# Row factors stored to DRAM in 20-byte runs or as one run, with natural rows interleaved by five

## The chip, the cores and the metric

One core of one Trainium2 chip runs the kernel. The metric is the device time of one execution in microseconds (us).

## The reference

The kernel computes one inference step of a one-layer hybrid decoder with 4096 prompt tokens and 64 sample tokens of width 1024. Only the first lines matter for the change:

```python
def _rmsnorm(x, g):
    xf = x.astype(jnp.float32)
    r = lax.rsqrt(jnp.mean(xf * xf, axis=-1, keepdims=True) + RMS_EPS)
    return (xf * r).astype(x.dtype) * g
...
    h = _rmsnorm(x, g_pre)
    z = h @ w_in
    cb, cc, ch, cg, q, k, v, ag, mq, mg = _split_cols(z)
```

Every token has one factor r, from the sum of its squares; h is the token times r times a gain per channel; z is its projection to 2816 columns. Three groups work on z (a gated short convolution, sliding-window attention with sinks, attention to 256 memory tokens); an output projection and a second norm follow.

## The kernel before

The 4160 tokens (64 of the sample, then 4096 of the prompt) are cut into eight blocks of 520. The input projection runs in three phases, each over all eight blocks and about one third of the columns. Products are made of f32 operands split into a high and a low part (`split`, L360 and L361; `product`, L370), blocks 0 and 1 of phase 0 by plain block products, the rest by a scheme of seven products in place of eight. The inputs x come transposed (`x_load`, L240): channels lie on partitions and tokens along the free axis.

**Row factors.** A sum over channels would be a sum over partitions there, so the factors come from a second read of x in natural order. A block has five tiles `nat` of 104 tokens by 1024 channels (`row_load`, L264 to L267, on the SP queue). `row_step` squares one tile on ScalarE and adds it up along the row (L278) into one column of a small tile `r` of 104 partitions by 5. After the fifth, GpSimd makes the five columns into factors (L284, L285). Column i, partition p belongs to token 104 i + p of the block.

The factors are wanted along the free axis, the same on all 128 partitions. There are two ways to it. Blocks 0 and 2 (`PLAIN_BLOCKS` is 2) go through TensorE: `rows_diag` spreads the factors over the diagonals of a tile (L297), `rows_product` multiplies it by ones (L306), and ScalarE copies the bank to a tile `rb` (L308). Blocks 1 and 3 to 7 go through DRAM: GpSimd stores `r` to `rowd` (L290), and four steps later `rows_load` on the SP queue reads it back to all partitions at once (L253). Block 0 is stored to `rowd` too: phase 1 reads `rowd` again for blocks 0 and 1.

VectorE multiplies by `rb`: the inputs (`scale`, L337), whose results are stored for the later phases; for blocks 0 and 1 it does that only in phase 1, and in phase 0 it multiplies their outputs z (L625).

**Order of the work.** The whole projection is recorded with the order of each engine as the program writes it. All of SP's loads stand in one queue and start in order. GpSimd issues in the first phase all stores (`store`, L166): the gates `md`, the attention operands `qd`, the scaled inputs `hd`, and the `rowd` stores among them. A store of GpSimd also waits for the store issued eight places before it, whose semaphore it takes over.

Of the kernel before, what the change touches and what calls it, by code (L numbers as in the profile page):

```python
# [20 lines left out]
NS = 64  # L21
# [23 lines left out]
PLAIN_BLOCKS = 2  # L45
# [7 lines left out]
def hybrid_layer(ctx: ExitStack, tc: tile.TileContext, a: dict):  # L53
    nc = tc.nc
    TE, V, S, G, DMA = nc.tensor, nc.vector, nc.scalar, nc.gpsimd, nc.sync
# [17 lines left out]
    rowd = [tc.dram_tile([2 * HW], F32, name=f"rowd{b}") for b in range(NBLK)]  # L73
# [170 lines left out]
    RG = 104  # L244

    rows = {}
    nat, sq, after_nat = {}, [0], [14]

    row_loads, row_spreads = [], {}

    def rows_load(b, again=False):
        rows[b] = (temp(f"rb{b}")[:, : 2 * HW] if again else natp.tile([P, 2 * HW], F32, tag="rb", name=f"rb{b}"))
        DMA.dma_start(rows[b], rowd[b].partition_broadcast(P))  # L253

    def row_load(j):
        if j < 5 * NBLK:
            g = RG * j - NS
            if 2 <= j < 10 or 12 <= j < 14:
                t = (wa if j < 7 or j == 12 else wb).tile([P, 2, 512], F32, tag="w", name=f"nat{j}")
                t = nat[j] = t.rearrange("p a n -> p (a n)")  # L260
            else:
                t = nat[j] = natp.tile([P, D], F32, tag="nat", name=f"nat{j}")
            if g < 0:
                DMA.dma_start(t[:NS], a["x_s"])  # L264
                DMA.dma_start(t[NS:RG], a["x_p"][: RG - NS, :])
            else:
                DMA.dma_start(t[:RG], a["x_p"][g : g + RG, :])  # L267

    def row_step():

        j = sq[0]
        if j == 5 * NBLK:
            return
        b, i = divmod(j, 5)
        if i == 0:
            nat["r"] = tiny.tile([P, 8], F32, tag="r", name=f"r{b}", bufs=3)
        r, t = nat["r"], nat.pop(j)
        S.activation(t[:RG], t[:RG], AF.Square, accum_out=r[:RG, i : i + 1])  # L278
        if j in (10, 11) or j >= 14:
            row_loads.append(after_nat[0])  # L280
            after_nat[0] += 1
        sq[0] += 1
        if i == 4:
            G.tensor_scalar(r[:RG, 0:5], r[:RG, 0:5], 1.0 / D, EPS, op0=ALU.mult, op1=ALU.add)  # L284
            G.tensor_tensor(r[:RG, 0:5], r[:RG, 0:5], mhalf[:RG, 0:5], op=ALU.pow)  # L285
            if b in (0, PLAIN_BLOCKS):
                nat["factors"] = r
            if b == PLAIN_BLOCKS:
                return
            G.dma_start(rowd[b].rearrange("(i p) -> p i", p=RG), r[:RG, 0:5])  # L290
            if b > 0:
                row_spreads[b] = 4

    def rows_diag():

# [6 lines left out]
    def rows_product(b):  # L302

        acc = rows[b]
        for half in range(2):
            TE.matmul(acc[:, half], ones[:RG], diag[:RG, HW * half : HW * half + HW], start=True, stop=True)  # L306
        rows[b] = natp.tile([P, 2 * HW], F32, tag="rb", name=f"rb{b}")
        S.copy(rows[b].rearrange("p (a n) -> p a n", a=2), acc)  # L308

    def row_queue():  # L310

        for j in row_loads:
            row_load(j)
        row_loads.clear()
        for b in [b for b, n in row_spreads.items() if n == 1]:
            rows_load(b)
        for b in list(row_spreads):
            row_spreads[b] -= 1
            if row_spreads[b] == 0:
                del row_spreads[b]  # L320
# [229 lines left out]
    def next_block(ph, b, p):  # L550

        nph, nb = (ph, b + 1) if b + 1 < NBLK else (ph + 1, 0)
        load = lambda o: lambda: x_of(nph, nb, o)
        ready = lambda o: lambda: x_ready(nph, nb, o)
        jobs = []
        if nph < 2:
            jobs += {0: "B11", 3: "B21 B12", 4: "B22"} .get(p, "").split() if ph == 0 else \
                    {0: "B11", 3: "B21", 4: "B12", 5: "B22"}.get(p, "").split()
            jobs = [load(o) for o in jobs]
        if ph == 0:  # L560
            jobs.insert(0, row_queue)
            if 1 <= p < 4:
                jobs.append(row_step)
        if p == 1 and nph == 1 and nb < PLAIN_BLOCKS:
            jobs.append(lambda: rows_load(nb, nb > 0))
        if nph < 2:
            jobs += [ready(o) for o in ({4: "B11", 5: "B21 B12", 6: "B22"} if ph == 0 else
                                        {4: "B11", 5: "B21", 6: "B12 B22"}).get(p, "").split()]
        if ph == 0 and 4 <= p < 6:
            jobs.append(row_step)  # L570
        if nph < 2:
            if p == 6:
                jobs.append(lambda: t_sum(nph, nb, "T1"))
        return jobs
# [53 lines left out]
    def plain_jobs(b, s):  # L628
# [16 lines left out]
            (0, 6): lambda: [*parts(1, "B11"), *row, *fills(1, "S1", "S4"), *sums(3, 0), *row],  # L645
            (0, 7): lambda: [*row, *fills(3, "S2", "S3"), lambda: rows_diag()],
            (1, 0): lambda: [*parts(1, "B21"), *row, *row, lambda: rows_bank(0), lambda: rows_product(0), *z_rows(0, 1)],
            (1, 1): lambda: [*z_rows(0, 0), *done(0, 1), *row, *row],
            (1, 2): lambda: [*parts(1, "B12"), *done(0, 0), *fills(3, "S1"), *row],
            (1, 3): lambda: sums(2, 0),  # L650
            (1, 4): lambda: [*row, lambda: rows_diag(), lambda: rows_bank(2), *parts(1, "B22"), *gains(2, "B11"), *sums(2, 1),
                             *fills(2, "S2")],
            (1, 5): lambda: [lambda: rows_product(2), *fills(2, "S3"), *row, *fills(2, "S1"), *gains(2, "B21"), *fills(2, "S4"),
                             *row],
            (1, 6): lambda: [*scales(2, "B11"), *gains(2, "B12"), *scales(2, "B21", "B12"), *row],
# [4 lines left out]
    def plain_loads(b, s):  # L660
        if s + b == 0:
            first_w("A22")
        for j in {(0, 0): (0,), (0, 1): (1,), (0, 2): (2, 3, 4), (0, 3): (5, 6, 7), (0, 4): (8, 9, 10), (0, 5): (11,),
                  (0, 7): (12, 13)}.get((b, s), ()):
            row_load(j)
        if (b, s) == (0, 1):
            first_w("A12")
        for nb, o in {(0, 1): [(0, "B12")], (0, 2): [(0, "B22")], (0, 3): [(1, "B11")], (0, 4): [(1, "B21")],
                      (0, 6): [(1, "B12")], (0, 7): [(1, "B22")], (1, 2): [(2, "B11")], (1, 3): [(2, "B21")],
                      (1, 4): [(2, "B12")], (1, 5): [(2, "B22")]}.get((b, s), ()):  # L670
            x_of(0, nb, o)
        row_queue()
# [1583 lines left out]
```

## Time and profile before

| what | value |
| --- | --- |
| runs | 1472.13, 1472.27, 1476.53 us; median 1472.27 |
| profiled execution, its own time | 1470.74 us |
| span of the profiled execution | 1469.0 us |
| granted TensorE clock | 0.999 of full speed |
| moved by DMA | 369.59 MB, mean 252 GB/s |
| stores to `rowd` | 7, of 2 KB each |

The profile is of one execution. The span runs from the first instruction to the last; the execution's own time is 1.74 us more. Busy time, waits and the chain of waits are read from that one execution: a row with "<-" names an engine and line that waited and what ended the wait; the three numbers behind it are the total in us, how often, and the longest. In rows of a tile, three durations are minimum, median and maximum in ns, with the start of the first and the last in us. In a window's row each engine has busy time and, in brackets, the instructions that touched the window; PE is TensorE, PEld its weight loads, DVE VectorE, ACT ScalarE and POOL GpSimd, and SPq a DMA queue of SyncE.

### The profile page before, as it was taken

What the parts mean: (1) busy time and instruction counts of PE and PEld (TensorE: products, weight loads), DVE (VectorE), ACT (ScalarE), POOL (GpSimd) and SP (SyncE); (2) the same over time, 40 slices, a digit from 0 to 9 for tenths busy, and PEclk for the clock granted to TensorE, in tenths of its full rate; (3) what the DMA queues carried; (4) which work ended last, traced back from release to release, by engine and by line L of the source; (5) the groups of instructions that cost most, each with busy time, mean ns of one, the idle gap of its engine ahead of it and who ended that gap; (6) DMA issues with size and microseconds to landing.
All of it is one profiled execution on the core that took longest, in us unless ns stands there. A gap on an engine that the chain in (4) does not pass through costs nothing.

```text
span 1469.0 us, 31997 instructions
## 1 busy us (share of the span) xinstructions
PE 1453.3 (99%) x11887; PEld 1342.3 (91%) x11887; DVE 1235.0 (84%) x1991; ACT 888.9 (61%) x2170; POOL 431.9 (29%) x544
## 2 busy tenths in 40 slices
PE   9999999999999999999999999999999999999997
PEld 9999999999999999999999999778888888888875
DVE  6779887899988888798677777899998999999975
ACT  6776565566532222244545444788888878888862
POOL 0222322312403474300021130234334333433452
PEclk9999999999999999999999999999999999999999
DMA  9999999887866676688897679997887788888876
GB/s 265 191 248 223 297 275 265 248 288 248 216 229 244 243 248 232 225 284 253 281 233 266 215 215 329 279 280 240 252 263 241 240 243 268 243 248 264 254 266 224
DMA packets 233744, 369.59 MB, mean 252 GB/s; under 512 B 38501, under 2 KB 144485, under 8 KB 233557
## 3 DMA queue, kind: packets, MB, share of 16 engines
q1 hardware_dynamic: 210549, 314.66, 69.4%
q0 software_dynamic: 22320, 51.84, 12.4%
q8 instruction: 94, 1.54, 0.5%
q10 hardware_dynamic: 720, 1.05, 0.2%
q14 instruction: 61, 0.50, 0.1%
HBM read 251.00 MB, written 117.46 MB: 251 GB/s over the span
## 4 chain that ended last, share of the span: by engine, by line
PE 89%; DVE 4%; DMA 3%; ACT 2%; issue 1%; POOL 0%; ACTq 0%; SPq 0%; DVEq 0%; POOLq 0%
PE c L370 54%; PE y_c L1701 20%; PE ws L1394 3%; PE wo L1508 2%; PE wo L1115 2%; PE xs L1441 2%; PE wo L1503 1%; PE wt L1461 1%; PE xt L1461 1%; PE mem_acc L797 1%; DMA md<-th 1%; DMA nat<-in_x_p 1%; DMA ws4A<-in_w_in 1%; PE y L2069 1%; DMA md<-cacc 0%
## 5 line engine op out<-in xcount | busy, mean ns | idle before, releaser
L377 DVE TENSOR_TENSOR z<-c,z 128x520 f32<-128x520 f32 (+1 forms) x308 | 193.8, 643 | 71.8 <-PE c L370 70.8
L1425 ACT ACTIVATE sm<-sm,wnm 128x129 f32<-128x129 f32 x240 | 93.5, 392 | 13.8 <-DVE wrd L1429 7.1
L1701 PE MATMUL y_c<-wob,rows 128*128 128x512 f32 x384 | 95.8, 396 | 0.4 <-ACT s L1739 0.4
L1701 PE MATMUL y_c<-woT,a 128*128 128x512 f32 x384 | 95.2, 395 | 0.0
L1701 PE MATMUL y_c<-woT,down 128*128 128x512 f32 (+1 forms) x396 | 95.2, 389 | 0.0
L1701 PEld LDWEIGHTS y_c<-wob,rows 128*128 128x128 f32 x384 | 70.6, 188 | 17.5 <-ACT wpt L1366 2.4
L1701 PEld LDWEIGHTS y_c<-woT,down 128*128 128x128 f32 x396 | 71.7, 188 | 15.8 <-DVE swnm L1996 0.4
L1701 PEld LDWEIGHTS y_c<-woT,a 128*128 128x128 f32 x384 | 70.6, 188 | 15.2
L1232 ACT ACTIVATE xp<-xs,xnm 128x256 f32<-128x256 f32 x128 | 59.9, 483 | 20.4 <-PE wo L1115 13.5
L918 POOL TENSOR_TENSOR os0T<-os0T,os1T 128x512 f32<-128x512 f32 x20 | 29.0, 1448 | 125.2 <-DMA os1T<-in_w_out 75.8
L411 ACT CAST zh<-z 128x520 fp32r<-128x520 f32 x56 | 33.3, 625 | 40.9 <-DVE z L377 32.9
L1394 PEld LDWEIGHTS ws<-ring,q 128*128 128x128 f32 (+1 forms) x480 | 48.6, 186 | 8.4 <-issue 1.2
L278 ACT ACTIVATE nat<-nat 104x1024 f32<-104x1024 f32 x40 | 42.3, 1057 | 23.0 <-DMA nat<-in_x_p 23.0
L1411 DVE COPY_PREDICATED sm<-wmask,ws 128x512 f32<-128x512 uint8 x60 | 43.7, 754 | 14.6 <-ACT sm L1405 14.6
L1455 ACT ACTIVATE xp<-xp,xrd 128x256 f32<-128x256 f32 x120 | 53.9, 503 | 2.1 <-DVE xrd L1238 1.1
L1394 PE MATMUL ws<-ring,q 128*128 128x256 f32 (+1 forms) x480 | 54.0, 294 | 1.1 <-issue 0.6
L1366 ACT COPY wpt<-wt 128x512 f32<-128x512 f32 x60 | 33.9, 593 | 27.4 <-PE wo L1508 27.4
L379 ACT COPY z<-c 128x520 f32<-128x520 f32 (+1 forms) x44 | 24.2, 553 | 43.0 <-PE c L370 40.0
L1701 PE MATMUL y_c<-woT,diag 128*128 128x512 f32 x192 | 48.8, 400 | 0.0
L1369 POOL TENSOR_SCALAR_AFFINE_SELECT wpt<-wpt 128x512 f32<-128x512 f32 x64 | 46.1, 740 | 7.0 <-ACT wpt L1368 6.9
L1641 POOL TENSOR_TENSOR yst<-yst,mhalf 128x1 f32<-128x1 f32 (+1 forms) x33 | 20.4, 617 | 93.7 <-DVE yst L1640 93.7
L166 POOL DMA_DIRECT2D md<-th x48 | 26.2, 547 | 67.6 <-DVE th L430 59.4
(1055 smaller groups left out, 5537.9 us busy)
## 6 DMA issues: line engine op xcount, KB each, us to landing
woT<-tdT SPq DMA_DIRECT2D x75, 512.0 KB
q<-qd SPq DMA_DIRECT2D x112, 192.0 KB
xr<-in_x_p SPq DMA_DIRECT2D x32, 512.0 KB
nat<-in_x_p SPq DMA_DIRECT2D x39, 416.0 KB
o_yp<-xr SPq DMA_DIRECT2D x31, 512.0 KB
md<-th POOLq DMA_DIRECT2D x48, 260.0 KB, 7.2
qd<-zh SPq DMA_DIRECT2D x48, 260.0 KB
qd<-z SPq DMA_DIRECT2D x42, 260.0 KB
```

The lines of the kernel that those rows point to most:

```text
L278: S.activation(t[:RG], t[:RG], AF.Square, accum_out=r[:RG, i : i + 1])
L370: TE.matmul(bank[:, :HW], l, r, start=first and i == 0, stop=last and i == 3 * KH - 1)
L377: add = lambda dst, other: V.tensor_tensor(dst, c, other, op=ALU.add)
L411: S.copy(hi, z)
L1232: S.activation(p[:, i, :], s[:, i, :], AF.Exp, bias=nm[:, i : i + 1], scale=SCALE, accum_out=den[:, i : i + 1])
L1366: S.copy(p3.rearrange("p h (r q) -> p r h q", r=2), t)
L1369: select = lambda out, step, op, slope: lambda: G.affine_select(out, p3, pattern=[[0, 4], [step, P]], compare_op=op, fill=0.0, base=0, cha ...
L1394: TE.matmul(out(kvh, col, bank), q(kvh, col, bank)[r], k(kvh, part)[r], start=first, stop=True, skip_group_check=not first, **place)
L1411: V.copy_predicated(self.of[i].sms[kvh][:, :, :P].rearrange("p (h a) k -> p a h k", a=2), third["wmask"].unsqueeze(1).to_broadcast([P, 2, ...
L1425: S.activation(sm[:, hh, :], sm[:, hh, :], AF.Exp, bias=nm[:, hh : hh + 1], scale=SCALE, accum_out=den[:, hh : hh + 1])
L1455: S.mul(p[:, i, :], p[:, i, :], self.rds[h][:, i : i + 1])
L1701: TE.matmul(self.acc[bank], self.parts[name][:, l, j], wo[o][j][:, r, cs], start=new and j + i == 0, stop=j == 3 and i == 2, skip_group_ch ...
```

## The change

It has three parts. For blocks 1 and 3 to 7 the five natural tiles no longer hold 104 consecutive tokens each: tile i takes tokens i, i+5, i+10 and so on, so that partition p of `r` holds the factors of the five neighbours 5p to 5p+4, and the store to `rowd` writes 104 runs of 20 bytes where it wrote 520 runs of 4 bytes. Blocks 0 and 2 keep the natural order, since their way through TensorE expects it. Block 0's copy in `rowd` is no longer written from `r` but from the first partition of the spread tile `rb`, as one run of 2080 bytes.

```diff
+    def spread(b):
+
+        return b not in (0, PLAIN_BLOCKS)
+
     def row_load(j):
...
                 DMA.dma_start(t[NS:RG], a["x_p"][: RG - NS, :])
+            elif spread(j // 5):
+                g = 5 * RG * (j // 5) - NS
+                DMA.dma_start(t[:RG], a["x_p"][g : g + 5 * RG, :].rearrange("(p i) d -> p i d", i=5)[:, j % 5])
             else:
                 DMA.dma_start(t[:RG], a["x_p"][g : g + RG, :])
...
-            if b in (0, PLAIN_BLOCKS):
+            if spread(b):
+                G.dma_start(rowd[b].rearrange("(p i) -> p i", i=5), r[:RG, 0:5])
+                row_spreads[b] = 4
+            else:
                 nat["factors"] = r
-            if b == PLAIN_BLOCKS:
-                return
-            G.dma_start(rowd[b].rearrange("(i p) -> p i", p=RG), r[:RG, 0:5])
-            if b > 0:
-                row_spreads[b] = 4
...
         S.copy(rows[b].rearrange("p (a n) -> p a n", a=2), acc)
+        if b == 0:
+            G.dma_start(rowd[b].unsqueeze(0), rows[b][:1])
```

On GpSimd, at the start of the program, before the change (`r0` and `r1` are the factors of blocks 0 and 1, `th` a gate):

```order
L284 TENSOR_SCALAR r0_501<-r0_501 104x5
L285 TENSOR_TENSOR r0_501<-r0_501,mhalf_68 104x5
L290 DMA rowd0_75<-r0_501 104x5x1
L284 TENSOR_SCALAR r1_700<-r1_700 104x5
L285 TENSOR_TENSOR r1_700<-r1_700,mhalf_68 104x5
L290 DMA rowd1_76<-r1_700 104x5x1
L166 DMA md_150<-th0_3_989 128x520
```

And the same place with the change (`rb0` is the spread tile of block 0):

```order
L291 TENSOR_SCALAR r0_501<-r0_501 104x5
L292 TENSOR_TENSOR r0_501<-r0_501,mhalf_68 104x5
L291 TENSOR_SCALAR r1_699<-r1_699 104x5
L292 TENSOR_TENSOR r1_699<-r1_699,mhalf_68 104x5
L294 DMA rowd1_76<-r1_699 104x5
L315 DMA rowd0_75<-rb0_941 13x1x40
L166 DMA md_150<-th0_3_989 128x520
```

Block 0's store has moved behind block 1's factors and their store, directly ahead of block 0's gate stores, and it reads one partition in 13 pieces of 40 numbers.

On GpSimd again, at block 6's factors, the rows before:

```order
L166 DMA hd5_B12_123<-place_160 128x1040
L284 TENSOR_SCALAR r6_2675<-r6_2675 104x5
L285 TENSOR_TENSOR r6_2675<-r6_2675,mhalf_68 104x5
L290 DMA rowd6_81<-r6_2675 104x5x1
L166 DMA md_150<-th4_2_2984 128x520
L166 DMA md_150<-th4_4_3001 128x520
```

And now:

```order
L166 DMA hd5_B12_123<-place_160 128x1040
L291 TENSOR_SCALAR r6_2675<-r6_2675 104x5
L292 TENSOR_TENSOR r6_2675<-r6_2675,mhalf_68 104x5
L294 DMA rowd6_81<-r6_2675 104x5
L166 DMA md_150<-th4_2_2984 128x520
L166 DMA md_150<-th4_4_3001 128x520
```

Nothing has moved here; only the form of the store differs, 104 runs of five numbers in place of 104 by 5 runs of one. On the other engines and on the SP queue the order is as before.

## Prediction

> **What bounds the kernel now.** The page comes first: its head and its row for TensorE.
>
> ```profile
> span 1469.0 us, 31997 instructions
> PE 1453.3 (99%) x11887; PEld 1342.3 (91%) x11887; DVE 1235.0 (84%) x1991; ACT 888.9 (61%) x2170; POOL 431.9 (29%) x544
> ```
>
> TensorE is busy for 1453.3 of 1469.0 us, so the whole kernel has 15.7 us in which it could start work sooner. The change touches only the first stage; the last product with a row factor starts at 382.5 us:
>
> ```profile
> L337 DVE TENSOR_TENSOR place<-place,rb x16: 1224/1233/1245, 94.7 to 382.5; 128x1040 f32<-128x1040 f32 x16
> ```
>
> So the second view is the windows of that stage, with columns for each engine's busy time, its instruction count, the granted clock, the DMA share and GB/s.
>
> ```profile
> core 0: us, PE busy (x) PEld busy (x) DVE busy (x) ACT busy (x) POOL busy (x), PEclk, DMA share, GB/s
> 0.00:20.00 20.00, 18.36 (x128) 17.74 (x129) 11.04 (x20) 11.57 (x22) 0.87 (x8) 1.00 0.90 274
> 20.00:60.00 40.00, 40.00 (x334) 39.88 (x334) 31.61 (x58) 31.74 (x63) 6.30 (x6) 1.00 0.98 221
> ...
> 100.00:140.00 40.00, 39.81 (x334) 39.60 (x334) 38.08 (x45) 27.40 (x49) 13.35 (x20) 1.00 0.93 241
> ...
> 180.00:220.00 40.00, 40.00 (x338) 40.00 (x337) 32.30 (x39) 23.07 (x39) 11.38 (x20) 1.00 1.02 270
> 220.00:260.00 40.00, 39.86 (x335) 39.65 (x333) 32.01 (x39) 24.56 (x43) 12.17 (x21) 1.00 0.99 268
> ...
> 300.00:340.00 40.00, 40.00 (x338) 40.00 (x337) 38.72 (x50) 27.36 (x49) 6.44 (x12) 1.00 0.77 244
> ```
>
> Two things stand here. The DMA engines are full (share 0.93 to 1.02) where the factors are made, which makes a cheaper store look promising. But TensorE does not wait for them: it runs 338 matmuls in 40 us at share 1.02 and the same 338 at share 0.77. What it loses after its start is 0.19 us (100 to 140) and 0.14 us (220 to 260). The waits of TensorE up to 420 us say the same:
>
> ```profile
> PE idle L707 <- POOL ident masks.py:199: 1.6, 1, 1.6
> PE c L370 <- DVE lo_2T L361: 0.2, 1, 0.2
> ```
>
> The 1.6 us lies before the first product and before any row factor exists; it stays.
>
> **The stores that change.** The third view is the tile `rowd`, the DRAM buffer of factors:
>
> ```profile
> L290 POOL DMA_DIRECT2D rowd<-r x7: 989/995/1192, 41.6 to 261.8; - x7
>   POOL md L166: 3.5, 1
> DMA to landing us min/median/max: 9.3/11.8/14.5
> ```
>
> Seven stores of 2 KB, each 520 runs of 4 bytes, take GpSimd about 1 us to issue and 9.3 to 14.5 us to land. Stage windows of 1 us around the store issued at 221.4 show what it does to everything else:
>
> ```profile
> 221.00:222.00 1.00, 1.00 (x11) 1.00 (x10) 0.72 (x2) 1.00 (x4) 0.70 (x2) 1.00 0.82 331
> ...
> 225.00:226.00 1.00, 1.00 (x11) 1.00 (x10) 1.00 (x2) 1.00 (x3) 0.00 (x0) 1.00 0.81 37
> 226.00:227.00 1.00, 1.00 (x11) 1.00 (x10) 1.00 (x2) 0.83 (x3) 0.00 (x0) 1.00 0.11 0
> 227.00:228.00 1.00, 1.00 (x10) 1.00 (x10) 1.00 (x3) 1.00 (x2) 0.42 (x1) 1.00 0.36 21
> 228.00:229.00 1.00, 1.00 (x11) 1.00 (x10) 1.00 (x2) 0.35 (x1) 1.00 (x3) 1.00 0.66 75
> ...
> 233.00:234.00 1.00, 1.00 (x11) 1.00 (x10) 0.99 (x2) 0.67 (x2) 0.72 (x2) 1.00 1.05 376
> ```
>
> From 225 to 229 us the core moves 37, 0, 21 and 75 GB/s where 331 and 376 stand on either side: a hole worth 4 - (37+0+21+75)/354 = 3.6 us of full traffic (354 is the mean of 331 and 376). That the tiny runs make it is my inference from its place, just behind the store; no row of this profile separates it from the transfers around it. TensorE's column stays at 1.00 through all of it.
>
> GpSimd's own timeline and the waits of GpSimd, ScalarE and the SP queue show who suffers:
>
> ```profile
> 221.40 0.99 POOL L290 DMA_DIRECT2D rowd<-r  x1 [0.30 <-POOL r L285]
> 222.39 1.11 POOL L166 DMA_DIRECT2D md<-th  x2
> ...
> 232.65 1.07 POOL L166 DMA_DIRECT2D md<-th  x2 [3.46 <-DMA rowd<-r]
> ```
>
> ```profile
> ACT nat L278 <- DMA nat<-in_x_p: 23.0, 11, 4.8
> ACT th L429 <- DMA md<-th: 16.3, 5, 5.0
> ```
>
> ```profile
> SPq L253 <- DMA rowd<-r: 4.4, 1, 4.4
> ```
>
> And the chain of waits shows how little of that reaches TensorE:
>
> ```profile
> 205.54 9.98 DMA nat<-in_x_p
> ...
> 222.39 10.92 DMA md<-th
> ...
> 233.33 0.30 ACT th L429
> ...
> 249.90 170.10 PE c L370 x1425
> ```
>
> One gate store queued right behind `rowd` takes 10.92 us to land, ScalarE waits for its buffer and goes on at 233.33, and what follows releases TensorE at 249.90. This is the one place where the chain through the factors reaches TensorE, and there it waited no more than the 0.14 us of its window.
>
> **The change part by part.** *Six stores in runs of 20 bytes (blocks 1, 3 to 7).* Runs fall from 520 to 104. For the price per run I take the nearest store of GpSimd, 128 runs of 2080 bytes:
>
> ```profile
> L166 POOL DMA_DIRECT2D md<-th x48 | 26.2, 547 | 67.6 <-DVE th L430 59.4
> ```
>
> ```profile
> md<-th POOLq DMA_DIRECT2D x48, 260.0 KB, 7.2
> ```
>
> (989 - 547) / (520 - 128) = 1.13 ns a run, so 104 runs take about 547 - 24 x 1.13 = 520 ns: 6 x 0.47 = 2.8 us less GpSimd work. GpSimd is 29% busy and off the path here, so this is worth nothing by itself. The hole, if it goes by the count of runs, falls to a fifth, 0.7 us: 6 x 2.9 = 17 us of transfer time comes free, the landing falls towards that of a gate store, 7.2 us in the median, and the waits 3.5 us (GpSimd), 4.4 us (SP) and part of ScalarE's 16.3 us go. What is late next is TensorE itself, which is already issuing at full pace; all of that becomes slack. To the end it brings from 0 to 0.19 + 0.14 = 0.33 us by the busy columns. By the counts, (338-334) + (338-335) = 7 matmuls of 40/338 = 0.118 us, it is 0.83 us. I take 0.4, between the two.
>
> The Trainium skill's "DMA: Bandwidth & Descriptors", section Specifications, speaks against the fifth: transfers under 512 B are read-modify-writes, and 20 bytes are as far under that line as 4. Read as one fixed penalty per store, the hole would stay 3.6 us and the term would be 0 in place of 0.4. The trace cannot decide it, since it has no store of 20-byte runs.
>
> *Block 0's store.* It moves from behind the factors of block 0 to behind the broadcast copy, past block 1's factors and store, and is now one run read from one partition. It waits for the copy on ScalarE; behind it on GpSimd stand the gate stores of block 0.
>
> ```profile
> L308 ACT COPY rb<-rows_y x2: 571/583/595, 58.3 to 84.7; 128x520 f32<-128x520 f32 x2
> ```
>
> ```profile
> 54.23 0.99 POOL L290 DMA_DIRECT2D rowd<-r  x1 [0.31 <-POOL r L285]
> ```
>
> ```profile
> 64.49 1.75 POOL L166 DMA_DIRECT2D md<-th  x3 [9.27 <-DVE th L430]
> ```
>
> The copy starts at 58.3 and ends at 58.9. GpSimd is idle from 55.2 until 64.49, so the store fits with 64.49 - 58.9 = 5.6 us to spare, less its issue (0.5 to 1.2 us). The copy's buffer is written again by the second copy at 84.7; even with the slowest landing seen, 58.9 + 1.2 + 14.5 = 74.6, it is read out 10 us before. The stored factors are wanted again only for block 0's second pass, whose first product starts at 329.4:
>
> ```profile
> L337 DVE TENSOR_TENSOR x_0B<-x_0B,rb x2: 1224/1226/1228, 329.4 to 336.0; 128x1040 f32<-128x1040 f32 x2
> ```
>
> Cost 0; without the idle time of GpSimd it would be the 58.9 - 55.2 = 3.7 us of its wait, on GpSimd and not on TensorE.
>
> *Interleaved natural rows (30 loads, blocks 1, 3 to 7).* Each of 104 partitions receives one row of 4 KB as before; only the distance between the rows in DRAM grows from 4 to 20 KB. Same bytes, same runs, same instructions on the SP queue. Nothing in the profile shows 4 KB rows at a 20 KB pitch, so the cost lies between 0 and a rival below; I take 0, as nothing in the run length changes, and a gain is excluded since contiguous rows are the easier case.
>
> **Sum.** Against the profiled execution, 1470.74 us (span 1469.0 and 1.74 around it): 1470.74 - 0.4 + 0 + 0 = 1470.3. That execution is 1.5 us below the median 1472.27 of the runs; against the median I forecast 1472.27 - 0.4 = 1471.9. A measurement of this kernel tells about 0.3% (4.4 us) from no change, so the forecast is "no difference".
>
> **Rivals.** *The holes stay* (0.22). If landing is set by a fixed receipt time and not by runs, nothing above shrinks: 1472.3. For it: a gate store with long runs needed 10.92 us as well (above). Against it: the hole and its place. The same page of the Trainium skill, section Anatomy of one DMA, gives a store through GpSimd about 2.0 us plus bytes over 436 GB/s, without a term for runs; by that rule `rowd` would land in an estimated 2.0 us, before and after alike. The 9.3 to 14.5 us here do not bear it out.
>
> *Slower: interleaved loads come late* (0.06). ScalarE already waits 11 times, 23.0 us, for natural rows, and being in order it then makes the split halves for TensorE late. At 249.90 TensorE has no cover. If a load took half as long again as the 9.98 us of the chain, TensorE would lose 5.0 us there: 1472.3 + 5.0 = 1477.3. It decides from 4.4 us more per load. Against it: runs stay at 4 KB, ScalarE is busy only 24.56 of 40 us in that window, and the load frees 3.6 us of hole for itself.
>
> *Faster: freed traffic speeds TensorE* (0.05). If the pace of matmuls hid waiting for full DMA engines, 17 us of free traffic could give 4.4 us or more, 37 matmuls of 0.118 us: 1467.9 or less. Against it stands 338 in 40 us at share 1.02 and at 0.77 alike.
>
> **How the numbers follow.** Forecast 0.67, holes stay 0.22, slower 0.06, faster 0.05. Both first cases are within 0.3%: 0.89. The range starts at 1469.5, about the profiled execution's 1470.74 less the upper bound of 0.83 and a little of the faster case, and ends at 1476.5, the slowest of the three runs, just below the slower case.
>
> **What would show it.** Right: the store's issue falls to about 0.5 us and its landing below 9.3 us; the windows behind a store no longer drop to 0 GB/s; the waits of 3.5 and 4.4 us on `rowd` are gone; TensorE's count stays at 338 in 40 us and its span within 1 us. Wrong in a step: holes of 3 us or more behind 20-byte stores; ScalarE's wait for natural rows above 23.0 us; GpSimd's gate stores of block 0 after 64.5 us. The forecast itself falls if TensorE's windows between 20 and 300 us change by more than 4.4 us in all.

## The result, and the profile after

| kernel | median us | lowest to highest | runs |
| --- | --- | --- | --- |
| before | 1471.80 | 1469.68 to 1476.53 | 8 |
| with the change | 1476.11 | 1474.94 to 1478.17 | 8 |

The ratio is 1.0028, with a 95% interval of 1.0017 to 1.0039: the change costs about 4.3 us. The profiled execution with the change took 1474.94 us (span 1473.2), against 1470.74 us (span 1469.0) before.

**What the change set out to do, it did.** The tile `rowd` in the profile after (starts in us, durations in ns, minimum, median and maximum):

```profile
L294 POOL DMA_DIRECT2D rowd<-r x6: 641/651/848, 53.6 to 260.3; - x6
L315 POOL DMA_DIRECT2D rowd<-rb x1: 543/543/543, 59.5 to 59.5; - x1
  ACT rb L313: 5.1, 1
DMA to landing us min/median/max: 2.1/4.0/8.0
```

The stores land in 2.1 to 8.0 us instead of 9.3 to 14.5. The windows after, of 40 us and, behind block 6's store, of 1 and of 15 us (columns as in the prediction):

```profile
20.00:60.00 40.00, 40.00 (x334) 39.88 (x333) 31.19 (x58) 31.77 (x63) 5.43 (x6) 1.00 0.94 228
100.00:140.00 40.00, 39.81 (x334) 39.60 (x333) 38.23 (x45) 27.84 (x50) 12.83 (x19) 1.00 0.77 235
220.00:260.00 40.00, 40.00 (x338) 40.00 (x337) 33.15 (x41) 24.48 (x43) 12.23 (x20) 1.00 0.88 276
300.00:340.00 40.00, 40.00 (x338) 40.00 (x338) 38.62 (x51) 27.36 (x49) 6.44 (x12) 1.00 0.76 242
340.00:380.00 40.00, 38.40 (x314) 37.52 (x313) 32.91 (x44) 21.53 (x37) 6.97 (x13) 1.00 0.79 274
...
224.00:225.00 1.00, 1.00 (x11) 1.00 (x11) 1.00 (x2) 0.52 (x2) 0.32 (x1) 1.00 0.25 87
...
228.00:229.00 1.00, 1.00 (x11) 1.00 (x10) 1.00 (x3) 1.00 (x2) 1.00 (x3) 1.00 0.29 97
...
220.00:235.00 15.00, 15.00 (x128) 15.00 (x127) 12.83 (x16) 9.31 (x14) 6.03 (x11) 1.00 0.83 264
```

The same 15 us behind the store, and the window 340 to 380 us, in the profile before:

```profile
221.00:236.00 15.00, 15.00 (x129) 15.00 (x128) 12.15 (x14) 8.84 (x16) 6.42 (x12) 1.00 0.98 201
...
340.00:380.00 40.00, 40.00 (x338) 40.00 (x337) 36.70 (x48) 24.88 (x44) 7.00 (x13) 1.00 0.84 285
```

The hole is gone but for two single microseconds at 87 and 97 GB/s. Over 15 us the core moves 264 GB/s instead of 201: 15 x 63 / 354 = 2.7 us of full traffic won behind one store, where the prediction expected 2.9. The gain is not of these two executions alone: from the full microsecond nearest the same store, 15 us hold 201 to 229 GB/s in five kernels with the 520-run store and 258 to 265 GB/s in six with the new one (the others come below). TensorE runs 338 matmuls from 220 to 260 us in place of 335, but the four kernels below that keep block 6's old store have 338, 338, 338 and 339, so these three matmuls are not shown to be a gain of the change.

**The loss lies after all that**, from 340 to 380 us: 314 matmuls in place of 338. There is no store of row factors in that stretch. By windows of 100 us, most of the balance is found there too. Before:

```profile
300.00:400.00 100.00, 100.00 (x841) 100.00 (x840) 95.42 (x126) 60.58 (x103) 31.14 (x38) 1.00 0.81 237
```

With the change:

```profile
300.00:400.00 100.00, 98.28 (x813) 97.19 (x813) 91.54 (x121) 59.07 (x101) 27.43 (x35) 1.00 0.76 224
```

28 matmuls of 100/841 = 0.119 us are 3.3 of the 4.2 us between the two spans. Matched one by one, TensorE's matmuls start 0.15 us later than before at 364 us and 3.9 us later at 412 us. GpSimd's timeline of that place shows the event. Before, the stores of block 7's gates:

```profile
341.00 0.55 POOL L166 DMA_DIRECT2D md<-th  x1 [2.98 <-DVE th L430]
342.22 1.15 POOL L166 DMA_DIRECT2D md<-th  x2 [0.67 <-DVE th L430]
343.38 0.54 POOL L166 DMA_DIRECT2D o_kp<-kl  x1
```

With the change:

```profile
341.16 0.54 POOL L166 DMA_DIRECT2D md<-th  x1 [2.98 <-DVE th L437]
342.37 0.54 POOL L166 DMA_DIRECT2D md<-th  x1 [0.67 <-DVE th L437]
345.61 0.55 POOL L166 DMA_DIRECT2D md<-th  x1 [2.69 <-DVE place L344]
346.16 0.54 POOL L166 DMA_DIRECT2D o_kp<-kl  x1
```

The second and third gate store followed each other directly; now there are 2.69 us of idle time between them. The named releaser (`place` on VectorE) cannot be it: the third store reads a gate tile `th`, as before, and VectorE had finished that tile by 342.7 us. How a pause of GpSimd reaches TensorE is read from the waits of the SP queue and of ScalarE, before:

```profile
SPq L194 <- DMA md<-th: 3.0, 1, 3.0
ACT w_0S L184 <- DMA wr_0S<-sd0S: 1.0, 1, 1.0
```

and with the change, with TensorE's row of waits:

```profile
SPq L194 <- DMA md<-th: 6.3, 1, 6.3
ACT w_0S L184 <- DMA wr_0S<-sd0S: 4.4, 1, 4.4
PE c L377 <- DVE lo_0T L368: 0.7, 1, 0.7
PE c L377 <- ACT w_0S L184: 0.5, 1, 0.5
```

L194 loads the weights of phase 1 into buffers that held block 7's gates, so the first weight load waits until block 7's last stores have landed: for the gates 6.3 us where it was 3.0. ScalarE, which splits the weights, waits 4.4 us where it waited 1.0, and TensorE, which never waited there before, now does. The stretch also loses traffic that cannot be bought back quickly. Windows of 3 us before:

```profile
344.00:347.00 3.00, 3.00 (x27) 3.00 (x26) 3.00 (x3) 1.50 (x4) 2.06 (x4) 1.00 0.86 309
...
356.00:359.00 3.00, 3.00 (x27) 3.00 (x27) 2.22 (x4) 0.18 (x1) 0.00 (x0) 1.00 0.45 176
```

and with the change:

```profile
344.00:347.00 3.00, 3.00 (x27) 3.00 (x26) 3.00 (x3) 1.28 (x3) 1.39 (x3) 1.00 0.18 62
...
356.00:359.00 3.00, 3.00 (x28) 3.00 (x27) 2.22 (x4) 0.03 (x1) 0.00 (x0) 1.00 1.03 396
```

62 GB/s in place of 309 while GpSimd pauses; the stores behind it then come bunched and keep the DMA engines full until 359 us, where before they had run out at about 357. The first weight load starts at 361.69 us (358.15 before).

### The profile page after: what moved, and what is told of

The parts are those of the page before. It is cut to its first block, busy times and chain, and to the rows that moved or that the text cites. A ratio compares the mean times of both kernels' runs of the same rounds, so it can differ in the third digit from the quotient of the medians.

```text
span 1473.2 us, 31998 instructions
## 1 busy us (share of the span) xinstructions
PE 1454.6 (99%) x11887; PEld 1342.8 (91%) x11887; DVE 1231.1 (84%) x1991; ACT 888.0 (60%) x2170; POOL 430.8 (29%) x544
## 3 DMA queue, kind: packets, MB, share of 16 engines
q0 software_dynamic: 22320, 51.83, 10.7%
q10 hardware_dynamic: 720, 1.05, 0.2%
## 4 chain that ended last, share of the span: by engine, by line
PE 85%; DVE 4%; DMA 4%; issue 3%; ACT 2%; SPq 1%; POOL 0%; ACTq 0%; DVEq 0%; POOLq 0%
PE c L377 51%; PE y_c L1708 20%; PE ws L1401 3%; PE wo L1515 2%; PE wo L1122 2%; PE xs L1448 2%; PE wo L1510 1%; PE wt L1468 1%; PE xt L1468 1%; PE mem_acc L804 1%; DMA vd<-v 1%; DMA ws10A<-in_w_in 1%; PE y L2076 1%; DMA x_1B<-in_xt 0%; DMA ring<-qd 0%
## 5 line engine op out<-in xcount | busy, mean ns | idle before, releaser
L1432 ACT ACTIVATION_READ_ACCUMULATOR sm<-sm,wnm 128x1 f32 x240 | 44.9, 187 | 0.0
L1228 DVE TENSOR_REDUCE xmx<-xs 128x2 f32<-128x512 f32 x64 | 43.5, 679 | 0.4 <-ACT xp L1239 0.3
```

The source lines that it names most:

```text
L1228: V.tensor_reduce(mx[:, :nb], s, axis=AX.X, op=ALU.max)
L1432: S.activation(sm[:, hh, :], sm[:, hh, :], AF.Exp, bias=nm[:, hh : hh + 1], scale=SCALE, accum_out=den[:, hh : hh + 1])
```

## The experiments

**The theory.** Before the change the same kind of pause stood elsewhere. Among GpSimd's waits of the kernel before is the row

```profile
POOL qd L166 <- issue: 1.9, 1, 1.9
```

and its timeline shows where, and that 11.50 us of idle time follow soon:

```profile
271.21 0.56 POOL L166 DMA_DIRECT2D qd<-zh  x1 [1.95 <-issue]
...
286.72 1.15 POOL L166 DMA_DIRECT2D sd6S<-ws6A  x2 [11.50 <-DVE ws6A L207]
```

It is the 89th store that GpSimd issues. With the change that pause is gone, and the one at the 116th has appeared. Theory A: the pause comes when a running count of what GpSimd's stores hand to each DMA engine passes 1024. I count, per engine, the runs of the store that go to it, and one more for its semaphore: 8 + 1 for a gate store of 128 runs, 40 + 1 for a row store of 520 runs, 7 + 1 for one of 104 runs, 1 + 1 for block 0's single run. The packets of GpSimd's queue bear out the shares of the row stores: each 520-run store left 16 packets of 160 bytes (40 runs of 4 bytes, more than 520 / 16 = 32.5; the trace does not say why), each 104-run store 14 packets of 140 bytes (7 runs of 20) and two smaller ones, and block 0's single run 13 packets of 160 bytes. Before, that gives 1016 after 88 stores and 1025 with the 89th; with the change 1022 after 115 and 1031 with the 116th. No row of the profile prints the running count (GpSimd's queue has 22,320 packets in both kernels), so it has to be tested. Under theory A the change costs time because cheaper stores fill the count more slowly, and carry the pause from a harmless place into the gate stores of block 7. Each ratio below is against runs of the kernel before on the same chip, with medians of 1470.09 to 1470.70 us.

The rivals: the interleaved loads cost (B), block 0's later store costs (C and F), the new parts cost only together (D), or the pause is a sign only (E).

**Block 0's store back to 520 runs.** All else as changed.

```diff
             else:
                 nat["factors"] = r
+                if b == 0:
+                    G.dma_start(rowd[b].rearrange("(i p) -> p i", p=RG), r[:RG, 0:5])
...
-        if b == 0:
-            G.dma_start(rowd[b].unsqueeze(0), rows[b][:1])
```

> The change with block 0's store put back: 520 runs of 4 bytes from r, ahead of block 1's factors; the other six stores in 20-byte runs and the interleaved loads stay. Theory A (a full ring of store descriptors): each store of GpSimd puts one descriptor per run and one for its semaphore on each DMA engine, 9 for 128 runs, and GpSimd pauses when a count of 1024 per engine is passed. In the changed kernel I count 1022 after 115 stores and 1031 with the 116th, the gate store that started at 345.61 after an unexplained pause of 2.69 us; before the change 1016 after 88 and 1025 with the 89th, which started at 271.21 after an unexplained 1.95 us. Block 0's 520 runs add 39 per engine (40 in place of 1), so the count passes 1024 at the 111th store, near 316.2 us, ahead of 14 us in which GpSimd is idle: no pause at 343 to 346 us, TensorE's waits near 365 us gone, time 1471 to 1473. Theory B (the interleaved loads cost): they are still there, time 1475 to 1477. Theory C (block 0's new store costs): it is gone, time 1471 to 1473, as in A.

Measured: 1469.81 us, ratio 0.9995 (0.9986 to 1.0004). The loss is gone. The pause stands where the count of 1016 after 110 stores puts it, at the 111th:

```profile
319.95 0.56 POOL L166 DMA_DIRECT2D vd<-v  x1 [2.46 <-issue]
332.39 0.54 POOL L166 DMA_DIRECT2D hd_B<-x_0B  x1 [11.89 <-DVE x_0B L344]
```

Behind it GpSimd would idle anyway: 11.89 us are left of that. But theory C, that block 0's store itself costs, expects the same time, so the next run separates them.

**An unread store added, of five runs per partition.** Nothing of the change is undone; the kernel gets more work.

```diff
+    pad = tc.dram_tile([P, 5, 256], F32, name="pad")
...
         if b == 0:
             G.dma_start(rowd[b].unsqueeze(0), rows[b][:1])
+            G.dma_start(pad[:, :, :P], ident.unsqueeze(1).to_broadcast([P, 5, P]))
```

> The change, and one store more that nothing reads: behind block 0's store GpSimd writes a constant tile to a spare DRAM buffer, five runs of 512 bytes on each of 128 partitions, 327 KB. Theory A (a full ring of store descriptors): it adds 5 x 8 + 1 = 41 per engine, so the count passes 1024 at the store of v near 316.2 us (the 112th store now), where GpSimd is idle for 14 us afterwards. The pause of 2.69 us ahead of the gate store at 345.61 is gone, and the time falls to 1471 to 1473 although work was added. Theories B (interleaved loads) and C (block 0's store): both are still there, and the time stays 1475 to 1478.

Measured: 1470.29 us, ratio 1.0 (0.9992 to 1.0009). Adding a store of 640 runs takes the loss away. GpSimd's timeline has the pause here:

```profile
318.23 0.55 POOL L167 DMA_DIRECT2D vd<-v  x1 [2.49 <-issue]
```

and the window from 300 to 400 us reads

```profile
300.00:400.00 100.00, 100.00 (x841) 100.00 (x841) 95.67 (x126) 61.19 (x103) 27.10 (x39) 1.00 0.81 246
```

The pause is at the kernel's 111th store (the added one not counted), and TensorE is back at 841 matmuls. B and C cannot explain that: the interleaved loads and block 0's new store are all still there.

**The same with one run per partition**, which moves the count by 9 only, as a control.

```diff
+    pad = tc.dram_tile([P, 1, 256], F32, name="pad")
...
+            G.dma_start(pad[:, 0, :P], ident)
```

> Control: the change, and one store more that nothing reads at the same place, but one run of 512 bytes per partition, 65 KB. Theory A (a full ring of store descriptors): it adds 8 + 1 = 9 per engine, so the count passes 1024 one gate store earlier, at 342.4 in place of 345.6 us, still in the close row of gate stores: a pause of 2 to 4 us from about 341.7 us, and a time of 1475 to 1478, no better than the change. If added stores as such helped (another order of semaphores, another timing), this one would help too: 1471 to 1473.

Measured: 1474.12 us, ratio 1.002 (1.0011 to 1.0029), a little under the expected time. The pause has moved by exactly one store, to the gate store just ahead:

```profile
345.15 1.09 POOL L167 DMA_DIRECT2D md<-th  x2 [3.30 <-issue]
```

TensorE has 822 matmuls from 300 to 400 us. So an added store as such does not help; where it puts the count does.

**The interleaved loads alone**, in the kernel before, with the old stores. The factors of blocks 1 and 3 to 7 then land on other tokens than they belong to.

```diff
+            elif j // 5 not in (0, PLAIN_BLOCKS):
+                g = 5 * RG * (j // 5) - NS
+                DMA.dma_start(t[:RG], a["x_p"][g : g + 5 * RG, :].rearrange("(p i) d -> p i d", i=5)[:, j % 5])
```

> The kernel before with the interleaved natural rows alone; the stores are as before, in 520 runs of 4 bytes, all seven. It leaves out the matching order of the store, so the factors of blocks 1 and 3 to 7 land on the wrong tokens; the amount of work is the same. Theory A (a full ring of store descriptors): the count is that of before, the pause falls at the 89th store near 271 us, time 1470 to 1473. Theory B (interleaved loads cost): time 1475 to 1477, and ScalarE's wait for natural rows above the 23.0 us of before. Theory C (block 0's new store): it is not there, time 1470 to 1473.

Measured: 1470.92 us, ratio 1.0 (0.9991 to 1.0009), with the pause of 1.95 us at the 89th store (270.38 us), as before the change. Rows of 4 KB at a pitch of 20 KB cost nothing that can be measured. ScalarE's wait for natural rows did not grow from the 23.0 us of before:

```profile
ACT nat L281 <- DMA nat<-in_x_p: 3.0, 4, 1.5
```

That it is shorter says nothing for the loads: with the old loads and 520-run stores this wait was 23.0 us before and 3.8, 11.1 and 18.4 us in three kernels below.

**The new stores with the old loads**, which leaves the factors of those blocks in the wrong order.

```diff
-            elif spread(j // 5):
-                g = 5 * RG * (j // 5) - NS
-                DMA.dma_start(t[:RG], a["x_p"][g : g + 5 * RG, :].rearrange("(p i) d -> p i d", i=5)[:, j % 5])
```

> The changed kernel without its interleaved loads: natural rows are read as before the change, and the stores stay as changed (104 runs of 20 bytes, block 0 as one run). It leaves the order of the factors in blocks 1 and 3 to 7 wrong; bytes, runs and times of the work are those of the changed kernel. Theory A (fewer descriptors move GpSimd's pause from the 89th store to the 116th, among the gate stores of block 7): the count is that of the changed kernel, so the pause stands again before the 116th store, near 345 us, 2 to 3.5 us long, TensorE has 805 to 825 matmuls in 300 to 400 us where 841 stood before the change, and the time is 1473.5 to 1477 us. Rival D (the loss needs the interleaved loads together with the new stores, since the loads alone cost nothing): 840 matmuls or so, and 1470 to 1472 us.

Measured: 1474.57 us, ratio 1.0024 (1.0015 to 1.0032), and the pause as in the changed kernel:

```profile
345.39 0.55 POOL L166 DMA_DIRECT2D md<-th  x1 [2.69 <-DVE place L341]
```

With 815 matmuls from 300 to 400 us, the stores alone bring the loss; D falls.

**Block 0's new store alone**, in the kernel before.

```diff
-            if b == PLAIN_BLOCKS:
+            if b in (0, PLAIN_BLOCKS):
                 return
...
         S.copy(rows[b].rearrange("p (a n) -> p a n", a=2), acc)
+        if b == 0:
+            G.dma_start(rowd[b].unsqueeze(0), rows[b][:1])
```

> The kernel before with one part of the change alone: block 0's factors go to DRAM from the spread tile as one run, all other stores are 520 runs of 4 bytes and all loads are as before. Per DMA engine its store counts 2 in place of 41, so the count after the 88th store is 977 in place of 1016, and 1024 is passed by the 94th store (the attention operand vd of block 6, near 274.7 us), behind which GpSimd is idle for some 11 us. Theory A: a pause of 1.9 to 2.8 us before that store, none before the 89th and none among block 7's stores; 838 to 842 matmuls in 300 to 400 us; 1469.5 to 1472 us. Rival F (block 0's later store is itself part of the loss): 1473 us or more.

Measured: 1470.92 us, ratio 1.0003 (0.9994 to 1.0012); F falls. From 300 to 400 us its profile has 836 matmuls, two fewer than I had put. The pause stands at the 94th store, the one named beforehand, with the idle time behind it that was expected to hide it:

```profile
278.82 0.55 POOL L166 DMA_DIRECT2D vd<-v  x1 [2.06 <-issue]
289.08 1.12 POOL L166 DMA_DIRECT2D sd6S<-ws6A  x2 [9.71 <-DVE ws6A L207]
```

**An unread store of two runs per partition**, to ask what the pause is: as the five-run edit, with 2 in place of 5.

> The changed kernel with an unread store of two runs of 512 bytes per partition behind block 0's store. It adds 17 to the count per DMA engine, so that 1024 is passed at the 114th store, near 341 us, when the store ahead of it (337.6 us) has had 3.5 us to land. What the pause consists of is asked. Theory A with a drain (GpSimd waits until the stores in flight have landed): hardly a pause at the 114th store, under 0.7 us beyond its wait for the gate, none at the 116th; 835 to 845 matmuls in 300 to 400 us; 1469.5 to 1472 us. Theory A with a fixed price: the pause stays 2 to 3.5 us and stands at the 114th store; the stores behind it come 1 us or more late; 825 to 838 matmuls; 1471 to 1474 us. If the pause stands at the 116th store still, the count is wrong and theory A with it.

Measured: 1473.83 us, ratio 1.0021 (1.0012 to 1.0029). The pause is at the 114th store, where the count puts it:

```profile
336.83 0.54 POOL L167 DMA_DIRECT2D hd_B<-x_0B  x1 [5.99 <-DVE x_0B L346]
342.95 1.63 POOL L167 DMA_DIRECT2D md<-th  x3 [5.58 <-DVE kl__4580 L422]
```

The two `hd_B` stores from 330 to 346 us, by the view of that tile:

```profile
DMA to landing us min/median/max: 3.0/3.2/3.5
```

And two windows:

```profile
341.00:344.00 3.00, 3.00 (x28) 3.00 (x27) 3.00 (x5) 1.60 (x2) 1.05 (x2) 1.00 0.00 0
...
300.00:400.00 100.00, 98.71 (x820) 97.67 (x819) 92.51 (x120) 59.53 (x102) 26.70 (x39) 1.00 0.79 234
```

That store waits 5.58 us, of which 2.98 belong to its gate (as in the kernels above): a pause of 2.60. Yet the store ahead of it, issued at 336.83, had landed by 336.83 + 3.5 = 340.3, and the core moved 0 GB/s from 341 to 344. My picture of a drain, that GpSimd waits for stores in flight, falls. The time came out at the upper edge of what a fixed price gave, with more matmuls lost (21) than the 3 to 16 I had put.

**A pause put in by hand** in the kernel before, ahead of the 116th store; descriptors and loads are unchanged.

```diff
+    dum = const.tile([P, 5], F32, name="dum")
+    G.memset(dum, 1.0)
...
+        if (b, idx) == (NBLK - 1, 6):
+            for _ in range(2):
+                G.tensor_tensor(dum, dum, dum, op=ALU.pow)
         store(md[idx, :, tokens(b)], th)
```

> The kernel before, with two powers over 128 x 5 numbers on GpSimd (about 1.5 us each by the factors' powers) ahead of block 7's gate store of index 6, the 116th store: a pause of about 3 us put by hand where the changed kernel has its own. Descriptors and transfers are those of the kernel before. Theory A (a pause there delays the stores behind it, the buffers and loads that wait for them, and in the end TensorE): block 7's stores start 2.5 to 3.5 us later, 805 to 830 matmuls in 300 to 400 us, 1473 to 1477 us. Rival E (the pause is a sign only; what costs is something else in the changed stores): 838 to 842 matmuls, 1470 to 1472 us.

The second run has 4 in place of 2:

> As the run with two powers, with four: a pause of about 6 us at the same store. Theory A: about 3 us more than with two, 780 to 805 matmuls in 300 to 400 us, 1476 to 1480.5 us. Rival E: 838 to 842 matmuls, 1470 to 1472 us.

Measured: 1476.92 us, ratio 1.0037 (1.0025 to 1.005), with two, and 1478.27 us, ratio 1.0047 (1.0034 to 1.006), with four. The powers took far longer than I had put. With two, the timeline and the window:

```profile
342.25 8.43 POOL L435 TENSOR_TENSOR dum<-dum 128x5 f32<-128x5 f32 x2
```

```profile
300.00:400.00 100.00, 96.19 (x793) 95.78 (x792) 89.74 (x117) 58.74 (x101) 34.50 (x36) 0.98 0.74 224
```

and with four:

```profile
344.64 10.93 POOL L435 TENSOR_TENSOR dum<-dum 128x5 f32<-128x5 f32 x4
```

```profile
300.00:400.00 100.00, 94.14 (x769) 93.60 (x768) 86.59 (x113) 58.24 (x104) 32.20 (x33) 0.97 0.70 226
```

So these are pauses of 8.4 and 10.9 us, not of 3 and 6, and they do not price 2.7 us directly. They show that time in which GpSimd issues no store at this very place costs TensorE matmuls, 48 and 72, without any change of a store. Not all of that is waiting: the granted clock is 0.5 for 3.41 us from 357.45 us with two powers and for 6.83 us from 359.16 us with four, by estimate 1.7 and 3.4 us, or 14 and 29 of the matmuls. The way to TensorE is another one as well, with two powers:

```profile
ACT v L422 <- DMA md<-th: 8.1, 1, 8.1
PE c L372 <- ACT hi_0T L362: 2.9, 1, 2.9
```

ScalarE waits for a gate's buffer, and from 352 us TensorE waits for the high part (`hi_0T`) that ScalarE makes next, while the first weight load waits only 2.3 us for the gates (2.2 us with four powers). E falls, but these runs do not show the way through the weight loads; that rests on the kernels of the table.

Put together, the pause and the loss by kernel (numbers of stores without the added ones; the store's ordinary wait for its gate taken off the pause, 0.67 us of 3.30 with one run and 2.98 of 5.58 with two):

| kernel | count before and with the store | store | pause us | matmuls, 300 to 400 us | ratio |
| --- | --- | --- | --- | --- | --- |
| before | 1016, 1025 | 89 | 1.95 | 841 | 1 |
| interleaved loads alone | 1016, 1025 | 89 | 1.95 | 840 | 1.0 |
| block 0's store alone | 1022, 1031 | 94 | 2.06 | 836 | 1.0003 |
| block 0's store as before | 1016, 1025 | 111 | 2.46 | 841 | 0.9995 |
| five runs added | 1018, 1027 | 111 | 2.49 | 841 | 1.0 |
| two runs added | 1021, 1030 | 114 | 2.60 | 820 | 1.0021 |
| one run added | 1022, 1031 | 115 | 2.63 | 822 | 1.002 |
| new stores, old loads | 1022, 1031 | 116 | 2.69 | 815 | 1.0024 |
| with the change | 1022, 1031 | 116 | 2.69 | 813 | 1.0028 |

All nine pauses stand at the store that passes 1024, and by this count the limit must lie above 1022 and at or below 1025. (The two kernels with powers, whose stores are those of before, have theirs at the 89th as well, 1.95 us each.) The waits behind it follow the table: in the four kernels with the loss, the first weight load waits 4.9 to 6.3 us for block 7's gates and ScalarE 3.8 to 4.6 us for the weights, in the five others 1.6 to 3.1 us and 0.5 to 1.3 us. The two kernels with the cheap stores and the pause out of the way (0.9995 and 1.0) gain nothing that can be measured: the cheaper stores are worth zero here, and where the pause goes the loss goes. No version beats the kernel before.

## Why the prediction was wrong

**The step that failed** is in the part on the six stores: "GpSimd is 29% busy and off the path here, so this is worth nothing by itself". It looks only at the places where the stores stand. (A later sentence there, "What is late next is TensorE itself, which is already issuing at full pace; all of that becomes slack", held at those places.) What the stores hand on is also a count, and with 33 fewer per engine at each of six stores and 39 fewer at block 0's, the count reaches its limit 27 stores later: at 345.61 us instead of 271.21. In the sum this is a missing term of +4.3 us, and by windows 3.3 us of it lie between 300 and 400 us.

**The row that was there.** The profile before had a wait of GpSimd of 1.9 us on "issue", with no releaser. The prediction did not weigh it, because nothing waited for it there: 11.5 us of idle time follow at 275 us. A harmless wait is a price whose place can change. GpSimd was off the path from 20 to 300 us, not among block 7's stores, where the weight loads of the next phase wait for the gates' tiles.

**The test watched the wrong stretch.** The prediction said that it falls if TensorE changes by more than 4.4 us between 20 and 300 us. It did not change there: the 40-us windows above hold 334, 334 and 338, where 334, 334 and 335 stood. The loss came at 340 to 380 us, where no changed store is issued and where the prediction therefore named nothing to look at.

**What held.** The landing fell below 9.3 us, the holes closed by about the size put (2.7 us of traffic against 2.9), and the waits on `rowd` of 3.5 and 4.4 us are gone. The whole of it was slack, as said: the term of -0.4 us cannot be told from 0 in the two runs with cheap stores and the pause out of the way, and the three matmuls from 220 to 260 us that it counted on come back with the old stores too. The rival in which the holes stay falls, and with it, for these stores, the prediction's other reading of one fixed penalty per store. The slower rival, late interleaved loads, falls (ratio 1.0 alone). The faster rival falls as well: TensorE has 338 matmuls in 40 us with the DMA share at 0.88 as at 1.02.

**What was mis-sized.** The issue of a store of 104 runs was put at 520 ns, on a line through the stores of 128 and 520 runs; it took 651 ns in the median, more than the 547 ns of 128 runs. The issue does not follow the number of runs alone. Block 0's store started at 59.52 us, after 5.06 us of waiting for the copy, and was done before the gates of block 0 at 64.86 us. That is 0.37 us later than before, and later than the 64.5 us at which the prediction would have doubted this step, but the gate store waited there for VectorE's `th` and not for the store.

**The line for no change** was put at 0.3%, or 4.4 us. The median moved 4.3 us and stays just under it, and inside the range; with 8 runs the interval leaves no change out all the same, so that line was too coarse for this kernel. That the median lies inside the range is luck: its upper end was the slowest of three runs and stood for no cost in the sum.

**What stays open.** What GpSimd does in the pause. It is no drain of stores in flight. Its length grows with the number of the store at which it comes: 1.95 us at the 89th, 2.06 at the 94th, 2.46 at the 111th, 2.69 at the 116th, which is 21.9 to 23.2 ns for each store issued so far. That fits a clean-up that goes through the earlier stores once; no run here varied the number of stores at a fixed count, so it is a reading and not shown. The profile before has one more idle time of GpSimd put down to "issue" that fits it: 1.96 us at 795.45 us, ahead of the 177th transfer that GpSimd issues, 88 after the first pause, which was as long after 88 stores. So the length would go by the transfers since the last pause and not by all of them. The count as made here stands at 1945 there and not at 2048, and three kernels (block 0's store as before, block 0's store alone, five runs added) have shorter gaps of 0.91 to 1.05 us, at the 183rd and 189th transfer, so what sets a second pause is open. The division of the 4.3 us between the late weight load and the bunched stores was not measured apart. With two runs added the last store (`vd`) was issued at 349.75 us, earlier than before (350.39), and most of the loss was there all the same, so it is not the issue of the last store that matters; the first weight load waited 5.7 us there for the gates to land.

## What to carry to other kernels

A store's pieces can have a cost that falls due far from the store: here GpSimd stops for 2 to 2.7 us at whichever store first takes their count past 1024 per DMA engine. So before calling saved stores "worth nothing", look for waits with no releaser among GpSimd's stores, work out where the edit moves them, and ask what is queued behind that store and whose buffers it frees. And when a kernel is slower in a stretch that the change does not touch, move the suspect by adding harmless work: a store that nobody reads told more here than undoing the change.

## What the runs showed of the hardware that was not expected

- GpSimd's pause by count: nine pauses at the store that passes 1024 by the count above, 1.95 to 2.69 us long, once with the DMA engines at 0 GB/s.
- The profile shows that pause as "issue" in some kernels and names an unrelated VectorE instruction in others (`place`, `kl`), so it is found by its place in the row of stores and not by its releaser.
- A power over 128 x 5 ones on GpSimd took 4.2 us each in a row of two and 2.7 us each in a row of four, where the powers of the factors (104 x 5) took 1.6 us.
